# Attention scores on the whole TensorE array from hi/lo parts, and one run of value matmuls per head pair

## The chip, the cores and the metric

The kernel runs on one core of a Trainium2 chip. The metric is the device time of one execution in microseconds (us). A core has TensorE (PE in the profile; PEld is its weight load), VectorE (DVE), ScalarE (ACT), GpSimd (POOL) and SyncE (SP), which here issues nearly all DMAs; sixteen DMA engines carry them. SBUF is the working memory with 128 partitions, PSUM takes the results of TensorE, and HBM is the main memory.

## The reference, cut to what matters

Two layers over 256 context and 2048 latent tokens of width 1024. In each layer one projection feeds four head groups; two of them are attention, each with 4 query heads of width 64:

```
c: banded attention, 2 K/V heads (each serves 2 query heads)
   block of 128 queries x (up to 384 neighbours + 256 context keys), plus one sink logit per head
d: 2-D neighbourhood attention, 4 K/V heads
   128 queries (8 rows x 16 columns) x (12 or 16 rows of 32 columns = 384 or 512 keys + 256 context keys)
p = softmax(q.k * scale + bias);  o = p.v
```

Q and K are RMS-normalised per head (c also rotated by position). All of it is float32.

## The kernel before

Tokens go through in nine sub-blocks of 256 (s = 0 is the context). `project` multiplies a sub-block with a 256-column chunk of the weights as three float32r matmuls per 128 rows (hi*hi, hi*lo, lo*hi: lines 220 to 222, 48 matmuls of 256 columns per projection). The chunk names are `ckv` (K and V of group c), `dk`, `dv`, `cq`, `dq`; the results are stored to scratch in HBM and read back by the attention. Per layer the sub-blocks come in three groups of three (T1, T2, T3); in each the order is `bv`, `ckv`, `dk`, `dv`, every chunk for all three sub-blocks. For Q and K, `normrope` (line 367) normalises into the tile `e`, and `store_t` (line 331) transposes it on TensorE into PSUM (`pst`), copies it on ACT into `th`, and stores it: `ckv` one DMA of 128 KB, `dk` one of 256 KB with 128 partitions as its outermost dimension, `dq` four of 64 KB. `dv` is stored by two DMAs per sub-block (line 320), whose destination is a pattern of 2 x 64 x 256 elements. The tiles `e` and `ev` share the tag "e" of the pool `ev`, `nsq`, `th` and `xo` the tag "sq"; each tag has two buffers, taken in turn, and a tile may be written once the reader of the buffer's last tile, here its DMA, is done. PSUM for the projections (`pp`) has two buffers.

Attention (line 1180) is a list of items, one per head and block of 128 queries: 144 in layer 0, 128 in layer 1. Their order is given in `trunk`: neighbourhood (`na`) row groups 3 and 2, the banded (`swa`) blocks 10 to 15, then na 0, swa 0 to 3, na 1, swa 4 to 9; projections and the output projection stand between them and fill TensorE. A software pipeline (`pipeline`) issues for item i its scores, for i-1 the exponential, for i-2 the transposes of the probabilities, for i-3 the values. `attend` (line 822) computes the scores with float32 operands on half arrays: local keys in rows 0 to 63, context keys in rows 64 to 127 (`tile_position`). The tile scheduler that builds the program sorts the instructions of each engine by its own estimate of times. `head_out` (line 904) multiplies probabilities and values for two heads at once, head 0 in columns 0 to 63 of the array, head 1 in columns 64 to 127 (line 921). The scheduler is free to put other matmuls between these. One float32 matmul leaves two records in the trace, a float32r matmul or a transpose one. K is loaded by POOL's queue, Q by `load_q` with two DMAs into the two halves of the partitions, the same values twice.

Of the kernel before, what the change touches and what calls it, by code (L numbers as in the profile page):

```python
# [37 lines left out]
class Kern:  # L38
# [238 lines left out]
    def project(self, L, name, s, h, w):  # L277
# [32 lines left out]
        if name in ("av", "bv"):  # L310
            nc.scalar.copy(e, ps)
            nc.sync.dma_start((self.sav if name == "av" else self.sbv)[s], e)
        elif name == "dv":
            nc.scalar.copy(e, ps)
            dst = self.svd[s * SUB:s * SUB + SUB]
            if s == 0:
                nc.sync.dma_start(dst.rearrange("(t p) d -> p t d", p=128), e)
            else:
                for t in range(2):
                    nc.sync.dma_start(dst.rearrange("(c r) d -> r c d", r=4)[2 * t:2 * t + 2], e[:, t])  # L320
        elif name == "ckv":
# [3 lines left out]
            self.store_t(e, "ckv", s)  # L325
        else:
            w = {"cq": self.wcq, "dq": self.wdq, "dk": self.wdk}[name]
            self.normrope(ps, e, 4, w, s if name == "cq" else None)
            self.store_t(e, name, s)

    def store_t(self, e, name, s):
# [12 lines left out]
        if s > 0 and name == "dq":  # L344
            for i in range(n):
                nc.scalar.copy(x[:, i].rearrange("p (g r c) -> p r g c", g=4, r=4), p[:, i].rearrange("p (r g c) -> p r g c", g=4, r=4))
        elif s > 0 and name == "dk":
            nc.scalar.copy(x.rearrange("p i (c r) -> p i r c", r=4), p.rearrange("p i (r c) -> p i r c", r=4))
        else:
            nc.scalar.copy(x[:, 0:n], p[:, 0:n])  # L350
        if name == "cq":
            nc.sync.dma_start(self.sqc.rearrange("(i p) t -> p i t", p=128)[:, :, tok], x)
        elif name == "ckv":
            nc.sync.dma_start(self.skc.rearrange("g d t -> (g d) t")[:, tok], x[:, 0])
        elif name == "dk":
            nc.sync.dma_start(self.skd.rearrange("(i h) d t -> (h d) i t", i=2)[:, :, tok], x)
        else:
            for h in range(2):
                v = x[64 * h:64 * h + 64]
                for i in range(2):  # L360
                    if s == 0:
                        nc.sync.dma_start(self.sqx[:, i, :, h].rearrange("t d c -> d t c"), v[:, i].rearrange("d (t c) -> d t c", t=2))
                    else:
                        half = ((s - 1) % 2) * 64
                        nc.sync.dma_start(self.sqd[(s - 1) // 2, i, :, :, h, half:half + 64].rearrange("g d c -> d g c"), v[:, i].rearrange("d (g c) -> d g c", g=4))
# [449 lines left out]
    def load_q(self, pool, src, n):  # L815
# [4 lines left out]
        return q  # L820

    def attend(self, pool, rc, q, parts, a0, n, bias, nsink=None, split=False):

        nc = self.nc
        p = self.pS.tile([128, 1024], F32, tag="s", name="pse")
# [5 lines left out]
        so, pi = S[:, 0:n], p[:, a0:a0 + n]  # L833
# [16 lines left out]
    def transpose_p(self, pool, S, n, rc=None):  # L850
# [6 lines left out]
        for c0 in range(0, n, 3):  # L857
# [39 lines left out]

    def load_v(self, pool, tag, src, n):
# [28 lines left out]
    def swa(self, L, pool, jobs):  # L927
# [3 lines left out]
        sqc, svc = self.sqc, self.svc  # L931
        skc = self.skc.rearrange("g d t -> d g t")
# [3 lines left out]
        def prep():  # L936
            n = 128 * (top - base + 1)
            k = st["k"] = pool.tile([128, 2, 1024], F32, tag="k", name="kst", bufs=2)
            nc.gpsimd.dma_start(k[64:128, :, 0:256], skc[:, :, 0:256])
            nc.gpsimd.dma_start(k[0:64, :, 0:n], skc[:, :, 256 + 128 * base:256 + 128 * base + n])  # L940
            st["vc"] = self.load_v(pool, "vc", svc[0:256].rearrange("(n p) d -> p n d", p=128), 2)
            st["v"] = {}

        def front(j, h):
            g = h // 2
            k, vc = st["k"], st["vc"]
            if h == 0:
                st[j] = self.load_q(pool, sqc.rearrange("(h d) t -> d h t", d=64)[:, :, (j + 2) * 128:(j + 3) * 128], 4)
# [6 lines left out]
            q = st[j][:, h]  # L955
# [5 lines left out]
            ctx = (1, 512, 768, k[64:128, g, 0:256])  # L961
            if j < 0:
                S, *f = self.attend(pool, rc[:, h % 2:h % 2 + 1], q, [ctx], 512, 256, self.cmask[:, 384:640], ns)
# [3 lines left out]
            a0 = 512 - (k1 - k0)  # L967
# [3 lines left out]
            S, *f = self.attend(pool, rc[:, h % 2:h % 2 + 1], q, [(0, a0, 512, k[0:64, g, k0:k1]), ctx], a0, 768 - a0, bias, ns, j == 15)  # L971
# [13 lines left out]
    def na(self, L, pool, rg):  # L985
# [3 lines left out]
        svd, sqd = self.svd, self.sqd  # L989
# [4 lines left out]
        def prep(hp):  # L994
            st[hp] = self.na_keys(pool, hp, 256 + 64 * r0, ng)

        def front(hp, cg, i):
            c0 = CG_COL[cg]
            k, vc = st[hp]
            if i == 0:  # L1000
                st["q"] = self.load_q(pool, sqd[rg, hp, cg], 2)
# [4 lines left out]
            vs, q, rc = st["v"], st["q"][:, i], st["rc"]  # L1006
# [5 lines left out]
            kl = k[0:64, i].rearrange("p (n q) -> p n q", q=256)[:, 0:3, 4 * c0:4 * c0 + 128]  # L1012
            parts = [(0, 128, 512, kl)]
            if ng == 4:
                parts.append((1, 512, 640, k[64:128, i, 256 + 4 * c0:256 + 4 * c0 + 128]))
            parts.append((1, 128 + nloc, 384 + nloc, k[64:128, i, 0:256]))
            S, *f = self.attend(pool, rc[:, i:i + 1], q, parts, 128, nloc + 256, pool_st["b", i][:, a0:768])
# [13 lines left out]
    def na_keys(self, pool, hp, t0, ng):  # L1031

        nc = self.nc
        kt = self.skd[2 * hp:2 * hp + 2].rearrange("h d t -> d h t")
        k = pool.tile([128, 2, 768], F32, tag="k", name="kst", bufs=2, padded_shape=[128, 2, 1024])
        nc.gpsimd.dma_start(k[64:128, :, 0:256], kt[:, :, 0:256])
        if ng:
            nc.gpsimd.dma_start(k[0:64], kt[:, :, t0:t0 + 768])
        if ng == 4:
            nc.gpsimd.dma_start(k[64:128, :, 256:512], kt[:, :, t0 + 768:t0 + 1024])  # L1040
        vc = self.load_v(pool, "vc", self.svd[0:256, hp * 128:hp * 128 + 128].rearrange("(n p) d -> p n d", p=128), 2)
        return k, vc

    def na_ctx_rows(self, L, pool):

        nc = self.nc
        st = {}

        def prep(hp):
            st[hp] = self.na_keys(pool, hp, 0, 0)  # L1050

        def front(hp, t, i):
            k, vc = st[hp]
            if i == 0:
                st["q"] = self.load_q(pool, self.sqx[t, hp], 2)
                st["rc"] = self.sm.tile([128, 2], F32, tag="rc", name="rc", bufs=4)
            rc = st["rc"]
            S, *f = self.attend(pool, rc[:, i:i + 1], st["q"][:, i], [(1, 512, 768, k[64:128, i, 0:256])], 512, 256, self.cmask[:, 384:640])
# [51 lines left out]
    def scratch(self, L):  # L1110
# [11 lines left out]
        self.sqc = self.scr(f"qc{L}", [256, NT * 128])  # L1122
        self.skc, self.skd = self.scr(f"kc{L}", [2, 64, NT * 128]), self.scr(f"kd{L}", [4, 64, NT * 128])
        self.sqx, self.sqd = self.scr(f"qx{L}", [2, 2, 64, 2, 128]), self.scr(f"qd{L}", [4, 2, 4, 64, 2, 128])
# [257 lines left out]
```

## Time and profile before

| | |
|---|---|
| time, median of 3 runs | 3062.85 us (3062.26 to 3063.51) |
| the profiled execution | 3059.56 us, of which the span of its instructions is 3057.7 us |
| mean granted TensorE clock | 0.959 |
| busy: PE, PEld, DVE, ACT, POOL | 93%, 80%, 53%, 35%, 27% of the span |
| DMA | 458 MB, mean 150 GB/s, queues busy 49% of sixteen engines' span |

Shares are averages over stages. The attention takes about 770 to 1470 us (layer 0) and 2312 to 2930 us (layer 1); the projections with the gated linear attention of group a lie before them. A PE row gives start, length and what it computed; rows of TensorE overlap, so the cost of a matmul is the distance from its start to the next start, not its length.

### The profile page before, as it was taken

The page shows a single profiled execution, that of the slowest core. Times are in us where ns is not written, and L with a number is a line of the kernel's source. Part 1 is how long each engine was busy: PE and PEld are TensorE (multiplying, and loading weights), DVE is VectorE, ACT ScalarE, POOL GpSimd, SP SyncE. Part 2 cuts the span into 40 slices and gives each one's busy share as a digit, 9 for nine tenths or more (in the row PEclk, how much of TensorE's full clock was granted, in tenths as well). Part 3 has the DMA queues.
Part 4 walks back from the last instruction along what each step waited for, and adds up shares of the span by engine and source line. Part 5 has one row for each costly group of instructions (what it writes and reads, how often), then busy time and mean ns, then how long its engine had stood idle before and what let it go on. Part 6 is the DMA issues. An engine that isn't in the chain of part 4 may idle for free. (4 is left out here: it accounts for less than half of the span.)

```text
span 3057.7 us, 56121 instructions
## 1 busy us (share of the span) xinstructions
PE 2854.0 (93%) x21206; PEld 2447.1 (80%) x21206; DVE 1618.5 (53%) x3741; ACT 1073.4 (35%) x2344; POOL 836.8 (27%) x922
## 2 busy tenths in 40 slices
PE   5989979978999999999979989999889999999998
PEld 5879879967777777777879889899778777777788
DVE  7554864475455444545654553465564546455453
ACT  3333323322343332434224323343223444343332
POOL 3242322343222111311132432333342213111132
PEclk9989979989999999999989899899999999999999
DMA  8634634254654263542554664242546643446365
GB/s 265 196 110 149 190 110 128 91 175 145 179 155 136 83 189 109 166 133 92 191 159 148 195 183 142 87 132 89 165 148 188 175 130 110 148 127 187 110 189 188
DMA packets 476684, 458.05 MB, mean 150 GB/s; under 512 B 54763, under 2 KB 355565, under 8 KB 476013
## 3 DMA queue, kind: packets, MB, share of 16 engines
q1 hardware_dynamic: 472782, 440.66, 47.2%
q0 software_dynamic: 3616, 13.64, 1.9%
q8 instruction: 173, 2.83, 0.4%
q14 instruction: 113, 0.93, 0.1%
HBM read 339.56 MB, written 114.60 MB: 149 GB/s over the span
## 5 line engine op out<-in xcount | busy, mean ns | idle before, releaser
L220 PE MATMUL ps<-whi,hh 128*128 128x256 f32 x1968 | 587.3, 298 | 33.6 <-ACT hh L258 18.2
L222 PE MATMUL ps<-whi,hl 128*128 128x256 f32 x1968 | 584.2, 297 | 9.1 <-DVE hl L259 9.1
L221 PE MATMUL ps<-wlo,hh 128*128 128x256 f32 x1968 | 583.1, 296 | 6.8 <-PEq L639 6.8
L213 POOL TENSOR_TENSOR wlo<-wraw,whi 128x512 fp32r<-128x512 f32 x208 | 284.7, 1369 | 831.3 <-ACT whi L212 801.9
L220 PEld LDWEIGHTS ps<-whi,hh 128*128 128x128 f32 x1968 | 393.0, 200 | 46.9 <-ACT hh L258 20.1
L220 PE MATMUL ps<-hh,whi 128*128 128x256 f32 x1376 | 405.6, 295 | 5.9 <-DVE nsq L376 2.6
L222 PEld LDWEIGHTS ps<-whi,hl 128*128 128x128 f32 x1968 | 391.9, 199 | 21.8 <-DVE hl L259 12.9
L221 PE MATMUL ps<-hl,whi 128*128 128x256 f32 x1376 | 405.9, 295 | 0.0
L221 PEld LDWEIGHTS ps<-wlo,hh 128*128 128x128 f32 x1968 | 393.0, 200 | 15.1 <-issue 12.8
L222 PE MATMUL ps<-hh,wlo 128*128 128x256 f32 x1376 | 404.5, 294 | 0.0
L844 ACT ACTIVATE S<-S,am 128x641 f32<-128x641 f32 (+5 forms) x272 | 226.0, 831 | 502.7 <-DVE am L836 490.3
L212 ACT CAST whi<-wraw 128x512 fp32r<-128x512 f32 x416 | 242.9, 620 | 428.1 <-DMA wraw<-w_in 193.4
L220 PE MATMUL pso<-mh,whi 128*128 128x256 f32 x1088 | 320.4, 295 | 7.3 <-DVE xo L1106 5.0
L222 PE MATMUL pso<-mh,wlo 128*128 128x256 f32 x1088 | 319.0, 294 | 3.0 <-POOL wlo L213 1.9
L221 PE MATMUL pso<-ml,whi 128*128 128x256 f32 x1088 | 318.4, 293 | 0.0
L221 PEld LDWEIGHTS ps<-hl,whi 128*128 128x128 f32 x1376 | 264.8, 192 | 35.8 <-issue 35.5
L220 PEld LDWEIGHTS ps<-hh,whi 128*128 128x128 f32 x1376 | 264.7, 192 | 32.2 <-issue 24.3
L222 PEld LDWEIGHTS ps<-hh,wlo 128*128 128x128 f32 x1376 | 264.4, 192 | 26.9 <-issue 26.5
L213 DVE TENSOR_TENSOR wlo<-wraw,whi 128x512 fp32r<-128x512 f32 x208 | 192.9, 931 | 170.4 <-ACT whi L212 162.2
L191 POOL TENSOR_TENSOR rs<-ms,mhalf 128x8 f32<-128x8 f32 (+2 forms) x140 | 172.1, 1231 | 314.6 <-DVE ms L189 305.6
L830 PE MATMUL pse<-kst,q 64*128 64x256 f32 (+2 forms) x1184 | 243.8, 457 | 3.2 <-DVE am L836 2.3
L220 PEld LDWEIGHTS pso<-mh,whi 128*128 128x128 f32 x1088 | 213.0, 196 | 25.4 <-issue 19.5
(203 smaller groups left out, 5052.8 us busy)
## 6 DMA issues: line engine op xcount, KB each, us to landing
wraw<-w_in SPq DMA_DIRECT2D x288, 256.0 KB
wraw<-w_out SPq DMA_DIRECT2D x128, 256.0 KB
adaw<-ada_w SPq DMA_DIRECT2D x82, 256.0 KB
scr_g<-ev SPq DMA_DIRECT2D x68, 256.0 KB
g<-scr_g SPq DMA_DIRECT2D x34, 512.0 KB
y<-scr_y SPq DMA_DIRECT2D x34, 512.0 KB
bias<-nbias SPq DMA_DIRECT2D x48, 256.0 KB
scr_h<-x SPq DMA_DIRECT2D x22, 512.0 KB
```

What stands on the lines that cost most here:

```text
L191: nc.gpsimd.tensor_tensor(out=rs, in0=ms, in1=self.mhalf.to_broadcast([128, n]), op=ALU.pow)
L212: nc.scalar.copy(hi[:, k], raw)
L213: (nc.gpsimd if i % 4 else nc.vector).tensor_tensor(out=lo[:, k], in0=raw, in1=hi[:, k], op=ALU.subtract)
L220: nc.tensor.matmul(out, ah(k), bh(k), start=(k == 0), stop=False)
L221: nc.tensor.matmul(out, ah(k), bl(k), start=False, stop=False)
L222: nc.tensor.matmul(out, al(k), bh(k), start=False, stop=(k == KB - 1))
L830: nc.tensor.matmul(p[:, lo:hi], q[r], k, start=True, stop=True, tile_position=(64 * o, 0))
L844: nc.scalar.activation(out=S[:, 0:w], in_=S[:, 0:w], func=AF.Exp, scale=-1.0, bias=m[:, 0:1], accum_out=m[:, 1:2])
```

## The change

Scores: `store_t` becomes `split_t`. ACT writes hi = float32r(x), VectorE writes lo = x - hi (tile `tl`, tag "e"), and both are stored, so the scratch arrays of Q and K double. In attention, K is loaded with its hi part in partitions 0 to 63 and its lo part in 64 to 127; Q's hi part stands twice in one tile (`qa`), its lo part twice in another (`qb`). Per head and key range there are two whole-array float32r matmuls, qa and qb, instead of one float32 matmul on half an array. Q is loaded into a staging tile (`qs`, 2 buffers) and copied by ACT into a float32r tile (3 buffers; 4 before).

Values: the chunks are taken in the opposite order with head 1 first, under high priority. The copies of the transposed probabilities go to DVE for head 0 and to ACT for head 1; before, the first three chunks went to DVE and the rest to ACT.

```
-        x = self.ev.tile([128, 2, 256], F32, tag="sq", name="th")
+        hi = self.ev.tile([128, 2, 256], F32R, tag="sq", name="th")
+        lo = self.ev.tile([128, 2, 256], F32R, tag="e", name="tl")
...
+                nc.scalar.copy(hv[:, i], pv[:, i])
+                nc.vector.tensor_tensor(out=lv[:, i], in0=pv[:, i], in1=hv[:, i], op=ALU.subtract)
...
-            nc.sync.dma_start(self.skc.rearrange("g d t -> (g d) t")[:, tok], x[:, 0])
-            nc.sync.dma_start(self.skd.rearrange("(i h) d t -> (h d) i t", i=2)[:, :, tok], x)
+        for l, x in zip(range(2), (hi, lo)):
+            elif name == "ckv":
+                nc.sync.dma_start(self.skc[:, l, :, tok], x[:, 0])
+            elif name == "dk":
                 for i in range(2):
+                    nc.sync.dma_start(self.skd[2 * i:2 * i + 2, l, :, tok], x[:, i])
...
-        q = pool.tile([128, n, 128], F32, tag="q", name="q", bufs=4, padded_shape=[128, 4, 128])
-        for o in range(2):
-            self.nc.sync.dma_start(q[64 * o:64 * o + 64], src)
+        q = pool.tile([128, 2, 2, 128], F32R, tag="q", name="q", bufs=3)
+        st = pool.tile([128, 2, 2, 128], F32, tag="ks", name="qs", bufs=2)
+        self.nc.sync.dma_start(st, src.rearrange("d h l t -> d (h l t)").rearrange("(o d) x -> o d x", o=1).to_broadcast([2, 64, 512]))
+        self.nc.scalar.copy(q, st)
...
+            q = pool.tile([128, 4, 128], F32R, tag="q", name="q", bufs=3)
+            st = pool.tile([128, 4, 128], F32, tag="ks", name="qs", bufs=2)
+            for o in range(2):
+                self.nc.sync.dma_start(st[64 * o:64 * o + 64], src(d))
+            self.nc.scalar.copy(q, st)
...
-        for o, lo, hi, k in parts:
-            r = slice(64 * o, 64 * o + 64)
-            nc.tensor.matmul(p[:, lo:hi], q[r], k, start=True, stop=True, tile_position=(64 * o, 0))
+        for lo, hi, k in ((a0, 512, kloc), (512, 768, kc)):
+            if hi > lo:
+                nc.tensor.matmul(p[:, lo:hi], qa[:, h], k, start=True, stop=False)
+                nc.tensor.matmul(p[:, lo:hi], qb[:, h], k, start=False, stop=True)
...
-            if c0:
+            if rc is not None:
                 nc.scalar.copy(pt[:, 0:w], p[:, 0:w])
...
-            for c in range(n):
-                for x, h in enumerate((r[6], r)):
-                    nc.tensor.matmul(py[64 * x:64 * x + 64, 0:128], h[2][c], h[5][0][c], start=(c == 0), stop=(c == n - 1), tile_position=(0, 64 * x))
+            with self.tc.high_priority():
+                for c in range(n - 1, -1, -1):
+                    for x, h in ((1, r), (0, r[6])):
+                        nc.tensor.matmul(py[64 * x:64 * x + 64, 0:128], h[2][c], h[5][0][c], start=(c == n - 1), stop=(c == 0), tile_position=(0, 64 * x))
...
-        self.skc, self.skd = self.scr(f"kc{L}", [2, 64, NT * 128]), self.scr(f"kd{L}", [4, 64, NT * 128])
+        self.skc, self.skd = self.scr(f"kc{L}", [2, 2, 64, NT * 128]), self.scr(f"kd{L}", [4, 2, 64, NT * 128])
```

On TensorE, in banded attention of layer 1 (`pse` scores, `ppt` transposes, `py` values, `ps` filling projections), the order before for one head pair's end:

```order
L830 MATMUL pse<-kst,q 128x384
L830 MATMUL pse<-kst,q 128x256
L220 MATMUL ps<-hh_31404,whi 128x256
L921 MATMUL py<-pt,vd 64x128 x5
L921 MATMUL py<-pt,vc 64x128
L221 MATMUL ps<-hl_31405,whi 128x256
L222 MATMUL ps<-hh_31404,wlo 128x256
L220 MATMUL ps<-hh_31404,whi 128x256
L221 MATMUL ps<-hl_31405,whi 128x256
L222 MATMUL ps<-hh_31404,wlo 128x256
L862 MATMUL ppt<-idn,S 128x128 x5
L921 MATMUL py<-pt,vc 64x128 x3
```

and now:

```order
L960 MATMUL py<-pt,vc 64x128 x4
L960 MATMUL py<-pt,vd 64x128 x8
L890 MATMUL ppt<-idn,S 128x128 x2
L857 MATMUL pse<-kst,q 128x384
L858 MATMUL pse<-kst,q 128x384
L857 MATMUL pse<-kc,q 128x256
L858 MATMUL pse<-kc,q 128x256
L890 MATMUL ppt<-idn,S 128x128 x3
```

The value matmuls of a pair, before in several runs with other matmuls between them, stand together; in the whole list there were 456 such runs, and there are 136, one for each pair. Both lists hold 1360 value matmuls.

On SP's queue, in group T2 of layer 1 (stores of K and V), before:

```order
L354 DMA scr_kc<-th 128x256
L356 DMA scr_kd<-th 128x2x256
L211 DMA wraw<-w_in 128x512 x4
L356 DMA scr_kd<-th 128x2x256
L469 DMA scr_so_6<-rec 128x512
L320 DMA scr_vd<-ev 2x64x256 x2
L356 DMA scr_kd<-th 128x2x256
L320 DMA scr_vd<-ev 2x64x256 x4
```

and now, from the stores of the last `ckv` sub-block to half of those of the second `dk` sub-block:

```order
L363 DMA scr_kc<-th 2x64x256
L363 DMA scr_kc<-tl 2x64x256
L366 DMA scr_kd<-th 2x64x256
L366 DMA scr_kd<-tl 2x64x256
L366 DMA scr_kd<-th 2x64x256
L366 DMA scr_kd<-tl 2x64x256
L211 DMA wraw<-w_in 128x512
L479 DMA scr_so_6<-rec 128x512
L211 DMA wraw<-w_in 128x512 x3
L366 DMA scr_kd<-th 2x64x256
L366 DMA scr_kd<-tl 2x64x256
```

Each `dk` sub-block now has four stores and each `ckv` sub-block two, all with the pattern 2 x 64 x 256 that only `dv` had.

On ACT, at the end of the same kind of group (T1 of layer 1), with the semaphores that an instruction waits for, now:

```order
L314 COPY ev<-ps 128x512 [waits DVE_49]
L353 CAST th<-pst 128x4x64 [waits DVE_49]
L471 COPY rec<-po 128x256 [waits PE_49]
L442 COPY ktt<-pk 128x256 [waits PE_49]
L314 COPY ev<-ps 128x512 [waits DMAHW4_49,DMAHW7_49,DMAHW1_49,DVE_49]
L314 COPY ev<-ps 128x512 [waits DMAHW2_49,DMAHW3_49,PE_49,Activation_49]
L212 CAST whi<-wraw 128x512
```

The second `dv` copy (the first line 314 with DMA waits) takes the buffer of the last `tl` and so waits for its stores; the weight casts of the next chunk stand behind it on ACT.

## Rows read from the trace of the kernel before

**Rows 1.** The page: engine busy us (share of the span) and instructions.
```profile
PE 2854.0 (93%) x21206; PEld 2447.1 (80%) x21206; DVE 1618.5 (53%) x3741; ACT 1073.4 (35%) x2344; POOL 836.8 (27%) x922
```

**Rows 2.** Stretches: length, then busy us (instructions) of each engine, clock, DMA share, GB/s.
```profile
766.00:932.00 166.00, 163.25 (x1259) 127.46 (x1258) 80.87 (x192) 67.49 (x150) 42.78 (x51) 0.98 0.60 169
...
2312.00:2470.00 158.00, 157.19 (x1228) 122.85 (x1228) 81.26 (x186) 69.14 (x151) 43.47 (x48) 1.00 0.66 187
2470.00:2584.00 114.00, 114.00 (x873) 86.11 (x872) 59.10 (x143) 46.62 (x110) 28.61 (x50) 1.00 0.37 106
```

**Rows 3.** Timeline of PE around one item's scores: start us, length us, instruction, count.
```profile
2493.33 0.28 PE L222 MATMUL ps<-hh,wlo 128*128 128x256 f32 x1
2493.54 0.91 PE L830 MATMUL pse<-kst,q 64*128 64x384 f32 x4
2494.38 0.39 PE L220 MATMUL ps<-hh,whi 128*128 128x256 f32 x1
2494.61 0.28 PE L221 MATMUL ps<-hl,whi 128*128 128x256 f32 x1
2494.72 0.29 PE L222 MATMUL ps<-hh,wlo 128*128 128x256 f32 x1
```

**Rows 4.** Timeline of PE around a run of one value matmul.
```profile
2496.22 0.27 PE L866 MATMUL ppt<-idn,rd 128*128 128x128 f32 x1
2496.43 0.43 PE L921 MATMUL py<-pt,vd 128*64 128x128 f32 x2
2496.79 0.39 PE L221 MATMUL ps<-hl,whi 128*128 128x256 f32 x1
2497.01 0.28 PE L222 MATMUL ps<-hh,wlo 128*128 128x256 f32 x1
```

**Rows 5.** Timeline of PE around a run of nine value matmuls.
```profile
2499.96 0.71 PE L862 MATMUL ppt<-idn,S 128*128 128x128 f32 x5
2500.59 0.76 PE L921 MATMUL py<-pt,vd 128*64 128x128 f32 x9
...
2501.20 0.70 PE L921 MATMUL py<-pt,vc 128*64 128x128 f32 x7
2501.83 0.39 PE L220 MATMUL ps<-hh,whi 128*128 128x256 f32 x1
2502.05 0.28 PE L221 MATMUL ps<-hl,whi 128*128 128x256 f32 x1
```

**Rows 6.** PE by line and shape: count, busy us, mean ns, idle before.
```profile
L830 PE MATMUL pse<-kst,q 64*128 64x384 f32 x480 | 219.6, 538 | 3.2 <-DVE am L836 2.3 <-DMA kst<-scr_kd 0.8
...
L830 PE MATMUL pse<-kst,q 64*128 64x256 f32 x576 | 184.0, 419 | 0.0
...
L830 PE MATMUL pse<-kst,q 64*128 64x128 f32 x128 | 31.1, 322 | 0.0
```

**Rows 7.** Stretches in the stores of K and V, columns as in rows 2.
```profile
604.00:605.00 1.00, 1.00 (x10) 1.00 (x10) 0.00 (x0) 0.00 (x0) 0.00 (x0) 1.00 0.91 198
606.50:611.50 5.00, 5.00 (x45) 4.97 (x44) 0.28 (x1) 0.36 (x1) 0.00 (x0) 1.00 0.14 48
...
1918.00:1947.00 29.00, 28.90 (x235) 27.73 (x234) 9.92 (x18) 10.46 (x20) 8.82 (x6) 1.00 0.29 94
```

**Rows 8.** What line 320 (the stores of `dv`) kept waiting: us, times.
```profile
  ACT ev L314: 5.5, 2
```

**Rows 9.** SP's queue in group T2 of layer 1: start us, length us, DMAs.
```profile
1918.70 0.37 SPq L356 DMA_DIRECT2D scr_kd<-th  x1
...
1935.62 0.38 SPq L356 DMA_DIRECT2D scr_kd<-th  x1
1938.69 5.18 SPq L320 DMA_DIRECT2D scr_vd<-ev  x4
```

**Rows 10.** Nearest operations to the added ones: ns min/median/max, first and last start.
```profile
L293 DVE SCALAR_TENSOR_TENSOR ev<-ev,ps x68: 660/686/690, 720.8 to 2752.8; 128x512 f32<-128x512 f32 x68
...
L212 ACT CAST whi<-wraw x416: 598/619/696, 8.4 to 3047.5; 128x512 fp32r<-128x512 f32 x139
```

More of the change, by code (lines that the diff above doesn't have):

```diff
@@ L324, in project @@
             self.normrope(ps[:, :, 0:128], e[:, :, 0:128], 2, self.wck, s)
-            self.store_t(e, "ckv", s)
+            self.split_t(e, "ckv", s)
         else:
@@ L328, in project, with split_t @@
             self.normrope(ps, e, 4, w, s if name == "cq" else None)
-            self.store_t(e, name, s)
-    def store_t(self, e, name, s):
+            self.split_t(e, name, s)
+    def split_t(self, e, name, s):
         nc = self.nc
@@ L341, in store_t @@
                 nc.tensor.transpose(p[:, i, t * 128:t * 128 + 128], e[:, t, i * 128:i * 128 + 128], self.idn)
-        x = self.ev.tile([128, 2, 256], F32, tag="sq", name="th")
+        hi = self.ev.tile([128, 2, 256], F32R, tag="sq", name="th")
+        lo = self.ev.tile([128, 2, 256], F32R, tag="e", name="tl")
         tok = slice(s * SUB, s * SUB + SUB)
-        if s > 0 and name == "dq":
+        if s > 0 and name in ("dq", "dk"):
+            if name == "dq":
+                hv, lv = (x.rearrange("p i (g r c) -> p i r g c", g=4, r=4) for x in (hi, lo))
+                pv = p.rearrange("p i (r g c) -> p i r g c", g=4, r=4)
+            else:
+                hv, lv = (x.rearrange("p i (c r) -> p i r c", r=4) for x in (hi, lo))
+                pv = p.rearrange("p i (r c) -> p i r c", r=4)
@@ L345, in store_t @@
             for i in range(n):
-                nc.scalar.copy(x[:, i].rearrange("p (g r c) -> p r g c", g=4, r=4), p[:, i].rearrange("p (r g c) -> p r g c", g=4, r=4))
-        elif s > 0 and name == "dk":
-            nc.scalar.copy(x.rearrange("p i (c r) -> p i r c", r=4), p.rearrange("p i (r c) -> p i r c", r=4))
-        else:
[L350 to L353, printed above, removed]
-            nc.sync.dma_start(self.skc.rearrange("g d t -> (g d) t")[:, tok], x[:, 0])
-        elif name == "dk":
-            nc.sync.dma_start(self.skd.rearrange("(i h) d t -> (h d) i t", i=2)[:, :, tok], x)
-        else:
-            for h in range(2):
-                v = x[64 * h:64 * h + 64]
-                for i in range(2):
[L361 to L365, printed above, removed]
@@ new lines, in split_t @@
+                nc.scalar.copy(hv[:, i], pv[:, i])
+                nc.vector.tensor_tensor(out=lv[:, i], in0=pv[:, i], in1=hv[:, i], op=ALU.subtract)
+        else:
+            nc.scalar.copy(hi[:, 0:n], p[:, 0:n])
+            nc.vector.tensor_tensor(out=lo[:, 0:n], in0=p[:, 0:n], in1=hi[:, 0:n], op=ALU.subtract)
+        for l, x in zip(range(2), (hi, lo)):
+            x = x.bitcast(F32)
+            if name == "cq":
+                nc.sync.dma_start(self.sqc[l].rearrange("(i p) t -> p i t", p=128)[:, :, tok], x)
+            elif name == "ckv":
+                nc.sync.dma_start(self.skc[:, l, :, tok], x[:, 0])
+            elif name == "dk":
+                for i in range(2):
+                    nc.sync.dma_start(self.skd[2 * i:2 * i + 2, l, :, tok], x[:, i])
+            else:
+                for i in range(2):
+                    for h in range(2):
+                        v = x[64 * h:64 * h + 64, i]
+                        if s == 0:
+                            nc.sync.dma_start(self.sqx[:, i, :, h, l].rearrange("t d c -> d t c"), v.rearrange("d (t c) -> d t c", t=2))
+                        else:
+                            half = ((s - 1) % 2) * 64
+                            nc.sync.dma_start(self.sqd[(s - 1) // 2, i, :, :, h, l, half:half + 64].rearrange("g d c -> d g c"), v.rearrange("d (g c) -> d g c", g=4))
@@ L896, in pipeline, with kv_tiles @@
                 res[i][3]()
+    def kv_tiles(self, pool, kt, vt, h0, t0, n):
+        kc = pool.tile([128, 2, 256], F32R, tag="kc", name="kc", bufs=2)
+        self.load_k(pool, kc, kt, h0, 0, 256)
+        kst = None
+        if n:
+            kst = pool.tile([128, 2, 1024], F32R, tag="kst", name="kst", bufs=2)
+            self.load_k(pool, kst, kt, h0, t0, n)
+        return kc, self.load_v(pool, "vc", vt[0:256, h0 * 64:h0 * 64 + 128].rearrange("(n p) d -> p n d", p=128), 2), kst
     def load_v(self, pool, tag, src, n):
@@ L930, in swa @@
         st = {}
-        sqc, svc = self.sqc, self.svc
-        skc = self.skc.rearrange("g d t -> d g t")
+        sqc, skc, svc = self.sqc, self.skc, self.svc
         lat = [j for j in jobs if j >= 0]
@@ L936, in prep @@
         def prep():
[L937 to L941, printed above, removed]
+            n = top - base + 1
+            st["k"] = self.kv_tiles(pool, skc, svc, 0, 256 + 128 * base, 128 * n)
             st["v"] = {}
@@ L954, in front @@
                             st["v"][b + x] = v[:, x]
-            q = st[j][:, h]
+            qa, qb = st[j]
             if h % 2 == 0:
@@ L988, in na @@
         st, pool_st = {}, self.bias
-        svd, sqd = self.svd, self.sqd
+        skd, svd, sqd = self.skd, self.svd, self.sqd
         r0, r1 = RG_ROWS[rg]
@@ L1029, in na @@
                 for a in ((hp, cg, i) for hp in range(2) for cg in range(4) for i in range(2))]
[L1031 to L1042, printed above, removed]
     def na_ctx_rows(self, L, pool):
```

56 lines of the change are left out of this document (30 added, 26 removed).

## The prediction

> **What bounds the kernel now.** I read four views in this order: the page, the stretches, the timeline of TensorE, the timeline of the stores. The page [rows 1] shows PE busy for 93% of the span, which alone says little. The stretches say more: in attention PE is busy 163.25 of 166, 157.19 of 158 and 114.00 of 114 us at a granted clock of 0.98 to 1.00 (the 2.4 GHz level), DVE and ACT about half of that [rows 2]. So there the sum of what stands in PE's list is the time, and work taken off that list comes straight off the end, as long as nothing else becomes late. The candidates for that are the DMA engines, at 0.60 and 0.66 in the neighbourhood stretches and 0.37 in a banded one.
>
> The timeline then gives the price of the two things that change. Filling matmuls start 0.11 to 0.12 us apart. From the last one before the scores (2493.33) to the second one after them (2494.61) are 1.28 us; less two ordinary distances the scores cost 1.04 us, although the array only streams 384 columns [rows 3]. A run of one value matmul costs 2497.01 - 2496.22 - 0.11 (transpose) - 0.12 = 0.56 us [rows 4]. A run of nine (eighteen records, two of the four rows of it are left out) costs 2502.05 - 2499.96 - 5 x 0.11 - 0.12 = 1.42 us [rows 5]; five transposes start 0.11 apart, (0.71 - 0.27)/4. Nine matmuls are five steps, as two heads' matmuls go side by side. So a run costs 0.345 us for entering and leaving the divided array, and 0.215 us a step.
>
> **The change part by part.** The trace's own execution is 3059.6 us; it is 3.3 us under the median of 3062.85, which I add at the end.
>
> *Scores.* 272 items, about 1.0 us each (items with context keys alone have less; their share is small [rows 6]): 272 us go. Added are whole-array float32r matmuls over 2 x (local + 256) columns: 176 items with 384 local keys, 64 with 512, 16 with 256, 16 with none, 348,160 columns in all. The nearest row is the filling float32r matmul of 256 columns at 0.12 us [rows 3], so 1360 x 0.12 = 163 us. Gain 109 us. 384 and 512 columns are not in the trace: at 0.11 per 256 the gain is 122, and if a wider float32r matmul fell back to what the old scores cost it is 0.
>
> *Values.* The PE lists have 456 runs with 827 steps before and 136 runs with 680 steps now. Before: 456 x 0.345 + 827 x 0.215 = 335 us; now 47 + 146 = 193 us. Gain 142 us. The reversed order of chunks means that a run waits once, for the last copy of head 1's probabilities, with the rest of PE's list queued behind it. PE's list has some ten or more fillers and the next scores between the last transpose and the run, over 2 us, against a copy of fewer columns than the 512 that take ACT 0.62 us [rows 10], so I cost that at nothing beyond the waits below.
>
> Together 251 us, 1.85 us for each of 136 head pairs.
>
> *Stores of K.* Here the change pays. The stores of `dv`, with a pattern of 2 x 64 x 256, run alone at a DMA share of 0.14, two of sixteen engines, and at 48 GB/s, though several are queued; one microsecond in which a `dk` store (128 partitions outermost) is in flight shows 0.91 and 198 GB/s [rows 7]. So patterns that begin with 2 all share the same two engines. `ckv` now makes two such stores (256 KB, 5.5 us at 48 GB/s) and `dk` four (512 KB, 10.9 us), `dv` two as before (5.5 us). In group T2 of layer 1 three `dk` start at 1918.70, and the second `dv` store follows at 1938.69 [rows 9], 20 us later. `tl` shares two buffers with `ev`, and the second `dv` copy takes the buffer of the last `tl`, so it now waits for three `dk` and one `dv` on those two engines: 3 x 10.9 + 5.5 = 38.2 us, about 5 us of other DMAs on them (0.29 of 20 us [rows 7], less their own part), and about 2 us to land (an estimate): 45 us, 25 late. Behind it on ACT stand the weight casts of the next chunk, and PE runs dry when its second PSUM buffer is full, one projection of 48 x 0.12 = 5.8 us later: 20 us. Before, such stores held ACT up for 5.5 us in all [rows 8]. The other five groups have the sub-blocks further apart or, in T1, a context sub-block without this pattern; I take 15 us each on average, 90 us, between 30 (only the backlog of the last stores counts) and 150 (25 each).
>
> *Loads of Q.* A neighbourhood pair's Q now comes in one DMA of 256 KB whose source begins with a repeat of 2. No row shows such a load. If it spreads like the others it costs nothing; if it goes like the stores with 2 in front it takes 5.5 us of two engines. I take the second, the row with the same leading 2. Row groups 3 and 2 stand together, 16 pairs: 88 us. The two engines also carry their sixteenth of all else: 0.60 x 166 = 100 and 0.66 x 158 = 104 us by busy share, or, at the 24 GB/s that one engine of the two moves, 169 x 166/384 = 73 and 187 x 158/384 = 77 us; I take 86 and 90. K, doubled, and the old Q loads, gone, cancel. Two loads land before the start (-11). That is 163 and 167 us, where PE would need 163 - 30 = 133 and 157 - 30 = 127: 30 and 40 us lost. In row groups 0 and 1 half of eight loads are issued in the banded stretch ahead, with its share of 0.37 [rows 2]: 5 us each for four. Sum 90 us; between 0 and 235 (no load early, shares as in rows 2: some 70 in each double stretch, 25 in each single one).
>
> The Trainium skill, "DMA: Bandwidth & Descriptors", section "Why a DMA increments its semaphore by 16 and not by 1", says that a DMA uses the largest number of engines, up to 16, that divides the outermost size (not 1) of both patterns, and its "Rules for kernel authors" name a leading repeat of c copies as confined to at most c engines. By this rule the two Q terms above hold; without it they are zero and the sum is 90 us lower. The trace agrees for the stores of `dv`: 48 GB/s at a share of 0.14.
>
> *Small things.* 70 subtractions on DVE at 0.69 us (48 us) and 136 Q copies on ACT at 0.62 us (84 us) [rows 10] lie beside PE, DVE being at 53% and ACT at 35% [rows 1]; where DVE leads, ahead of attention, some of the 48 shows: 10 us, between 0 and 48. The first scores of a Q tile now wait for DMA, then ACT, then PE, and the score bank still has one buffer: 15 us of new waits, between 0 and 40.
>
> Sum: 3059.6 - 109 - 142 + 90 + 90 + 15 + 10 = 3014; with 3.3 for the median **3017 us**, 1.5% faster: a gain of 251 of which 205 is given back to two DMA engines and small waits.
>
> **The rivals.** *A: the two-engine transfers hide.* For it: `dv` stores of this kind held up only 5.5 us in all [rows 8], Q has five buffers on its way, and the wait for a store costs only if PE has nothing else. Against it: before, one chunk in four did it, now three. With the Q loads hidden 3017 - 90 = 2927, with the stores hidden too 2837; I take 2910 as its middle.
>
> *B: slower, the two engines lead.* Place: the groups T1 to T3 and the double neighbourhood stretch. Price: 150 for the stores, some 160 for Q (half the early loads do not come early, and every other DMA of SP's queue passes the same two engines and arrives late), 25 for small things: 335 - 251 = 84 slower, 3147; it decides from a loss of 251 on. For it: SP and ACT take their work in order, so one late store stops weights and Q as well. Against it: late transfers also thin out what the two engines have to carry.
>
> *C: the scores do not get cheaper*, because wide float32r matmuls cost as much as the old ones: 3017 + 109 = 3126. *D: gain and loss cancel* within 0.2%, 6 us, about what a measurement of this kernel can tell from no change.
>
> **How the numbers follow.** Forecast 0.45, its own range 2960 to 3056 (the terms for stores and Q some 40 us either way). A 0.20, B 0.25, C 0.03, D 0.07. Faster: forecast and A, 0.65. Same: most of D, 0.06. Slower: B, C and the rest, 0.29. For 8 in 10 the range leaves out half of A below and a third of the slower cases above: 2895 to 3125.
>
> **What would show it.** In the new profile the scores should stand in four records per item at 0.15 to 0.18 us apart for 384 columns, with no gap to the fillers, and values in one run of 1.4 to 1.7 us. Stretches with only `dk` stores should show a share near 0.14 and 48 GB/s for 10 us and more; ACT's `ev` copy and DVE's `tl` should wait for stores; PE's idle time should grow between 150 and 620 and in the same part of layer 1. If a neighbourhood stretch of 16 pairs takes about 135 us instead of 165, Q's loads are spread or hidden, and A is right; if it takes over 190, B. The prediction is wrong at its root if PE is still near 100% busy in attention and the total is not shorter there.

## The result and the profile after

The changed kernel takes 3179.57 us (median of 4 runs, 3175.36 to 3186.22) against 3063.18 for the kernel before: the ratio is 1.0381, 95% interval 1.0362 to 1.0400. It is 3.8% slower. I had forecast 3017, 1.5% faster, with a range to 3125; rival B (slower, two engines lead) stood at 3147 with a chance of 0.25.

The page of the changed kernel, first line, as in [rows 1]:

```profile
PE 2695.1 (85%) x21078; PEld 2530.5 (80%) x21078; DVE 1619.3 (51%) x3835; ACT 1146.6 (36%) x2504; POOL 837.2 (26%) x914
```

PE has 159 us less to do (2854.0 before), in a span that is 115.5 us longer: it is not the work that grew but the gaps. Gaps between the starts of PE's matmuls that are longer than 0.7 us, less an ordinary 0.12 us each, sum to 204 us before and 491 now. PE's list itself became as short as forecast. Its timeline around one item's scores (start, length, instruction, count):

```profile
1063.30 0.36 PE L222 MATMUL ps<-hh,wlo 128*128 128x256 f32 x1
1063.50 0.34 PE L857 MATMUL pse<-kst,q 128*128 128x384 f32 x1
1063.67 0.34 PE L858 MATMUL pse<-kst,q 128*128 128x384 f32 x1
1063.85 0.28 PE L857 MATMUL pse<-kc,q 128*128 128x256 f32 x1
1063.97 0.28 PE L858 MATMUL pse<-kc,q 128*128 128x256 f32 x1
1064.09 0.28 PE L220 MATMUL ps<-hh,whi 128*128 128x256 f32 x1
1064.20 0.28 PE L221 MATMUL ps<-hl,whi 128*128 128x256 f32 x1
```

Matmuls of 384 columns start 0.17 to 0.18 us apart, those of 256 columns 0.12. From the last filler to the second one after are 0.90 us; less two ordinary distances 0.66, where [rows 3] had 1.04. And a pair's values, one run:

```profile
1061.66 0.28 PE L221 MATMUL ps<-hl,whi 128*128 128x256 f32 x1
1061.87 0.66 PE L960 MATMUL py<-pt,vc 128*64 128x128 f32 x8
1062.35 0.82 PE L960 MATMUL py<-pt,vd 128*64 128x128 f32 x12
1063.11 0.44 PE L890 MATMUL ppt<-idn,S 128*128 128x128 f32 x2
```

Twenty records (ten matmuls, five steps) take 1063.11 - 1061.66 - 0.11 = 1.34 us, where the forecast had 1.42.

The time went into gaps at the two places that rival B names, and at a third, the single row groups. First the stores of K. Stretches of the changed kernel in group T3 of layer 0, where the stores of `dk` run and those of `dv` queue behind them, columns as in [rows 2]:

```profile
655.00:660.00 5.00, 3.06 (x26) 2.77 (x24) 0.56 (x3) 0.00 (x0) 0.00 (x0) 1.00 0.14 50
660.00:665.00 5.00, 0.00 (x0) 0.00 (x0) 0.00 (x0) 0.00 (x0) 0.00 (x0) 0.67 0.14 48
665.00:670.00 5.00, 2.86 (x13) 2.86 (x14) 0.00 (x0) 0.58 (x1) 0.00 (x0) 0.50 0.14 48
```

Ten microseconds and more at a share of 0.14 and 48 GB/s, as with `dv` alone in [rows 7], and in the middle of it the busy time of every engine in the row is 0.00. Behind the gap PE's granted clock is 0.50, the 1.2 GHz level, so a gap costs more than its length.

Second, attention. I count from the start of an item's exponential to that of a later item's, so the items between are the same in every kernel. The filling matmuls among them are not: the three stretches hold 526, 550 and 505 before, 567, 594 and 580 in the change, so 5 to 9 us of the change's stretches, at 0.11 to 0.12 us a matmul, are more filling work. The stretches are items 0 to 31 and 40 to 71 of layer 0 (the double neighbourhood stretch; row group 0 with the banded items that lead to it) and the first 32 items of layer 1. Before:

```profile
775.00:936.00 161.00, 158.25 (x1221) 122.21 (x1221) 81.84 (x192) 67.39 (x150) 41.47 (x47) 0.98 0.59 169
974.00:1136.00 162.00, 157.39 (x1153) 117.43 (x1152) 75.80 (x173) 61.66 (x144) 27.39 (x49) 0.97 0.45 133
2323.00:2476.00 153.00, 153.00 (x1197) 117.48 (x1196) 82.55 (x191) 69.93 (x153) 42.39 (x48) 1.00 0.64 182
```

The same items in the changed kernel:

```profile
861.00:1028.00 167.00, 144.03 (x1199) 135.47 (x1200) 81.17 (x201) 77.94 (x169) 42.26 (x46) 0.92 0.64 187
1062.00:1229.00 167.00, 138.27 (x1204) 131.27 (x1204) 76.56 (x179) 68.61 (x158) 31.99 (x49) 0.90 0.55 158
2445.00:2617.00 172.00, 144.96 (x1203) 136.33 (x1204) 79.99 (x196) 79.95 (x174) 42.97 (x47) 0.92 0.64 189
```

PE was nearly full there; now it is idle for 23, 29 and 27 us, and its clock lower, so each stretch is longer although its scores and values take less. The mean DMA share, 0.55 to 0.64, shows no full engine: it is a mean over sixteen. Who waits for whom, from the waits of the changed kernel (us, times, longest):

```profile
DVE S L864 <- DMA bias<-nbias: 107.9, 29, 10.7
ACT q L835 <- DMA qs<-scr_qd: 64.9, 11, 11.2
ACT ev L314 <- DMA scr_kd<-tl: 57.4, 5, 13.7
DVE tl L354 <- DMA scr_kd<-tl: 30.8, 5, 8.2
```

The third and fourth line are the waits that the prediction named for the stores. The first is the telling one: the largest wait is not for Q but for the bias, a load that the change did not touch. Before:

```profile
DVE S L836 <- DMA bias<-nbias: 7.5, 3, 5.0
```

### The profile page after: what moved, and what is told of

It reads as the page before. It is cut to its first block, busy times and chain, and to the rows that moved or that the text cites. A ratio compares the mean times of both kernels' runs of the same rounds, so it can differ in the third digit from the quotient of the medians.

```text
span 3173.2 us, 56054 instructions
## 1 busy us (share of the span) xinstructions
PE 2695.1 (85%) x21078; PEld 2530.5 (80%) x21078; DVE 1619.3 (51%) x3835; ACT 1146.6 (36%) x2504; POOL 837.2 (26%) x914
## 5 line engine op out<-in xcount | busy, mean ns | idle before, releaser
L220 PE MATMUL ps<-whi,hh 128*128 128x256 f32 x1968 | 601.5, 306 | 100.1 <-ACT ev L314 44.2
L222 PE MATMUL ps<-whi,hl 128*128 128x256 f32 x1968 | 594.9, 302 | 12.4 <-DVE hl L259 12.4
L221 PE MATMUL ps<-wlo,hh 128*128 128x256 f32 x1968 | 592.8, 301 | 4.6 <-PEq L649 3.8
L220 PEld LDWEIGHTS ps<-whi,hh 128*128 128x128 f32 x1968 | 407.5, 207 | 112.0 <-ACT ev L314 46.0
L222 PEld LDWEIGHTS ps<-whi,hl 128*128 128x128 f32 x1968 | 405.5, 206 | 18.1 <-DVE hl L259 15.5
L221 PEld LDWEIGHTS ps<-wlo,hh 128*128 128x128 f32 x1968 | 407.6, 207 | 7.4 <-issue 4.2
L890 PE MATMUL ppt<-idn,S 128*128 128x128 f32 x1360 | 250.7, 287 | 103.0 <-DVE pt L900 45.6
L220 PEld LDWEIGHTS ps<-hh,whi 128*128 128x128 f32 x1376 | 272.3, 198 | 4.7 <-DVE nsq L386 3.3
L221 PEld LDWEIGHTS ps<-hl,whi 128*128 128x128 f32 x1376 | 272.0, 198 | 1.3 <-issue 1.1
L890 PEld LDWEIGHTS ppt<-idn,S 128*128 128x128 f32 x1360 | 161.7, 145 | 128.9 <-DVE pt L900 48.6
```

The source lines that it names most:

```text
L220: nc.tensor.matmul(out, ah(k), bh(k), start=(k == 0), stop=False)
L221: nc.tensor.matmul(out, ah(k), bl(k), start=False, stop=False)
L222: nc.tensor.matmul(out, al(k), bh(k), start=False, stop=(k == KB - 1))
L890: nc.tensor.transpose(p[:, i], S[:, (c0 + i) * 128:(c0 + i + 1) * 128], self.idn)
```

## The experiments

The theory: DMAs whose pattern begins with 2 all run on the same two engines, and what is late is everything that passes them. The main rival: the new chains (DMA, ACT, PE ahead of the scores; ACT's last copy ahead of the values) make PE wait, whatever engines carry the data.

**a1_q64.** Q's loads as two DMAs of 64 partitions:

```
-        self.nc.sync.dma_start(st, src....to_broadcast([2, 64, 512]))
+        for o in range(2):
+            self.nc.sync.dma_start(st[64 * o:64 * o + 64], src)
```

> The changed kernel with each neighbourhood load of Q made as two DMAs of 64 partitions in place of one whose source begins with a repeat of 2; nothing else differs. Theory (the DMAs that begin with 2 crowd two engines): attention, which did not get shorter, loses most of its idle time, some 150 to 200 us: 2980 to 3030. Rival 1 (only the stores of K count): within 15 us of 3180. Rival 2 (the added chain DMA, ACT, PE ahead of the scores and the single run of values make PE wait, whatever engines carry the load): within 30 us of 3180, with the same idle time in attention.

Measured 2981.57 us (2975.69 to 2985.05), 198 less than the change. The stretches of the same items:

```profile
845.00:986.00 141.00, 135.35 (x1224) 128.08 (x1224) 83.15 (x204) 79.49 (x172) 43.37 (x46) 1.00 0.86 236
1019.00:1151.00 132.00, 128.04 (x1185) 122.21 (x1185) 74.02 (x180) 68.48 (x157) 31.49 (x49) 1.00 0.70 198
2333.00:2471.00 138.00, 134.19 (x1216) 127.16 (x1217) 82.72 (x196) 80.59 (x175) 43.45 (x47) 1.00 0.88 247
```

The three are 26, 35 and 34 us shorter (their filling matmuls differ by 2 us of work at most), PE is idle for only 4 to 6 us of each at a clock of 1.00, and the DMA share has gone *up*, to 0.70 to 0.88, with the same bytes in less time. The wait for the bias, untouched here too, falls from 107.9 to 32.8 us:

```profile
DVE S L865 <- DMA bias<-nbias: 32.8, 13, 4.3
ACT q L836 <- DMA qs<-scr_qd: 31.0, 10, 6.4
```

Rivals 1 and 2 of this run fall.

**a2_k64.** K's stores of 64 partitions:

```
-                nc.sync.dma_start(self.skc[:, l, :, tok], x[:, 0])
+                for h in range(2):
+                    nc.sync.dma_start(self.skc[h, l, :, tok], x[64 * h:64 * h + 64, 0])
...
-                for i in range(2):
-                    nc.sync.dma_start(self.skd[2 * i:2 * i + 2, l, :, tok], x[:, i])
+                for h in range(2):
+                    nc.sync.dma_start(self.skd[h::2, l, :, tok].rearrange("i d t -> d i t"), x[64 * h:64 * h + 64])
```

> The changed kernel with the stores of the parts of K made per head of 64 partitions (four DMAs per dk step as before the edit, four for ckv where it has two) in place of patterns that begin with 2. Theory: the groups T1 to T3 of both layers lose the lag that they gained, 70 us in each layer: about 3040; attention stays as it is. Rival 1 (the stores hide, Q counts): within 15 us of 3180. Rival 2 (the lag in these groups comes from 70 added subtractions and copies on DVE and ACT): within 30 us of 3180.

Measured 3057.04 us (3048.28 to 3068.88), 122.5 less. The first exponential of layer 0 starts at 797 us, against 861 in the change (775 before); from the last one of layer 0 to the first of layer 1 it is 838 us, against 891 (851 before). Attention keeps its losses, 166, 167 and 175 us for the three stretches. Both rivals of this run fall; the theory's 3040 was 17 us low. The wait behind the third line above falls to 15.9 us:

```profile
ACT ev L314 <- DMA scr_kd<-tl: 15.9, 4, 5.5
```

**a3_q64_k64.** Both edits.

> Both of these edits. Theory: the sum of the two gains, about 2850 (the list of PE is 250 us shorter, minus some 25 us of new waits and 15 for DVE and ACT), idle time of PE back near the 204 us that the kernel before has in gaps. Rivals that leave the cost to the new chains: above 3100.

Measured 2884.37 us (2881.39 to 2888.20), ratio to before 0.9426 (0.9411 to 0.9442). The rivals fall; the time is 34 us above the theory's number. PE's gaps sum to 257 us, still above the 204 of before. Behind Q's fix, K's is worth 97 us; behind K's, Q's is worth 173.

**a4_values** and **b1_scores64**, the two halves of the change apart. The first is the kernel before with the edit of the values:

```
-            for c in range(n):
-                for x, h in enumerate((r[6], r)):
+            with self.tc.high_priority():
+                for c in range(n - 1, -1, -1):
+                    for x, h in ((1, r), (0, r[6])):
...
-            if c0:
+            if rc is not None:
```

The second is a3 with exactly that edit undone.

> The kernel before with the edit of the values alone (one run per head pair, last chunk first, all copies of head 1's probabilities on ACT); its scores, Q and K are as before. Theory (a run costs 0.345 us to enter and leave plus 0.215 a step): 142 us less, about 2920. Rival (the run waits for its last copy and PE with it, so what is saved on entering is idle instead): 3040 to 3080.

> The scores alone with all transfers spread: the changed kernel with 64-partition Q loads and K stores, and with the values' runs and copies as they were before. Theory (the two parts add): the values alone took 85 us off the kernel before, all together 174, so the scores should be worth 89 here: about 2969. By the prediction's sum for the scores (109 less 25 of small waits) 2974. Rival (the two parts overlap, either one alone frees the same wait of DVE's reduction for the score bank): below 2940 here, since each alone would then be worth more than in the sum.

Values alone: 2973.02 us (2965.34 to 2978.72), 85 less than before, where theory had 142 and the rival none. Scores alone, with spread transfers: 2971.80 (2959.29 to 2975.59), 82.5 less. The two parts add: 167.5 us apart, 174 together; b1's rival (below 2940) falls. I summed PE's list in the attention stretches of the kernel before and of these two (each run from the end of the filler ahead to the filler behind, the median of each shape by its count): the values go from 323.5 to 176.9 us, the scores from 276.7 to 161.5. So the list shrinks by 147 and 115 us, as the sum had it (142 and 109); 62 and 32 us of it don't reach the end. For the values, the waits of PE itself (us, times, longest) in the run with the values alone show where most of it stands:

```profile
PE pse L830 <- DVE am L836: 21.3, 16, 4.1
PE py L922 <- ACT pt L870: 9.7, 6, 2.5
PE ppt L862 <- DVE pt L872: 9.5, 4, 5.7
PE ppt L862 <- DVE rc L847: 6.3, 3, 3.4
```

In the kernel before, the first of these reads

```profile
PE pse L830 <- DVE am L836: 2.3, 3, 1.0
```

and the other three come to 0.6 us. So 19 of the 62 us are waits of the scores for their bank, 15 waits of the transposes, and 10 the run of values waiting for ACT's last copy. PE, quicker by a run, seems to come back before DVE has read out the one score bank; that is a reading of these waits, not a test of it.

**b2_addq** and **b2_addq16.** The kernel before, with only the suspected cost added: 256 KB more per Q load, into a tile that nothing reads, once with a repeat of 2 in front, once in 64-partition DMAs:

```
+        if n == 2:
+            z = pool.tile([128, 512], F32, tag="qz", name="qz", bufs=2)
+            for o in range(2):
+                self.nc.sync.dma_start(z[:, 256 * o:256 * o + 256], src.rearrange("d h t -> d (h t)")....to_broadcast([2, 64, 256]))
```

> The kernel before with only the suspected cost added: beside each neighbourhood Q load two more DMAs of 128 KB whose source begins with a repeat of 2, into a tile that nothing reads. No engine waits for the data; only SP waits for the two buffers. Theory (two engines are filled and all else that passes them comes late): 80 to 160 us slower than before, 3140 to 3220, with idle time of PE in attention, where there was next to none. Rival 1 (what hurt was the wait for Q itself, on ACT, ahead of the scores): within 20 us of 3058. Rival 2 (any 256 KB more per pair would do it, bytes and not engines): as slow as the run with the same bytes in 64-partition DMAs.

> The control to that: the same 256 KB more per pair into the same unread tile, as four DMAs of 64 partitions. Theory: within 15 us of 3058. Rival 2 (bytes): as slow as its sister.

With two in front 3331.01 us (3329.25 to 3335.90), ratio 1.0909 (1.0880 to 1.0937): 277 slower, far more than expected. With the same bytes spread 3072.11 (3071.02 to 3079.20), 18 slower, a little over the 15 expected. Both rivals fall: nobody needs these data, and the bytes are the same. What waits, in the first:

```profile
DVE S L840 <- DMA bias<-nbias: 158.0, 18, 30.3
ACT ev L292 <- DMA scr_g<-ev: 115.6, 5, 51.2
```

and in the second:

```profile
DVE S L840 <- DMA bias<-nbias: 22.3, 12, 5.6
ACT ev L292 <- DMA scr_g<-ev: 4.1, 4, 2.7
```

Other transfers come late, one of them by 51 us. Why this costs more than the change's own Q loads isn't settled. The engines' work doesn't explain it: the added loads have 1 KB packets, twice as many as the change's, and all packets of that size together took 3109 us for 2292 before, which is 6.0 us of each of the two engines for one pair, against 5.8 in the change (b3 below). But this run adds a second cost, which its expectation mentions and does not price: SP itself stood for the two buffers of the added tile, and behind it every later load of its queue,

```profile
SPq L823 <- DMA qz<-scr_qd: 71.9, 33, 3.9
```

against 2.5 us in 4 times at the same line of the second. How much of the 277 us that is, no run separates.

**b3_q2act.** a2 with Q's loads in the change's form, from ACT's queue (`nc.scalar` for `nc.sync`).

> The changed kernel with spread K stores, and the Q loads with the repeat of 2 as in the change but issued from ACT's queue in place of SP's. Theory (the pattern picks the engines, the queue does not matter): within 30 us of the run with spread K stores alone, 3057. Rival (SP's queue, in which each such load holds up the next transfers in order): most of 170 us comes back, 2880 to 2930.

Measured 3055.22 us (3049.13 to 3069.47), a2's time. The order of SP's queue doesn't set the time; the rival falls. It does set who waits: the bias, 110.9 us in a2, waits less, and ACT's copy of Q, 77.4 us in a2, more:

```profile
ACT q L836 <- DMA qs<-scr_qd: 87.4, 18, 11.7
DVE S L865 <- DMA bias<-nbias: 45.7, 14, 7.3
```

So much of the bias's lateness seems to have come through SP's queue, behind Q's loads. And as these loads now have a queue of their own, the page prices them (packets, MB, share of 16 engines):

```profile
q10 hardware_dynamic: 8840, 17.83, 1.6%
```

1.6% of 16 x 3058 us is 783 us of engine, by two engines and 68 loads 5.8 us a load; the sum had 5.5.

**c1_qkv64, c2_copies, c3_allact, c4_bufs.** a3 with the stores of `dv` spread too; that with the copies of the probabilities as before the change; with all of them on ACT; and c1 with a buffer more for Q and for its loads:

```
                 for t in range(2):
-                    nc.sync.dma_start(dst.rearrange("(c r) d -> r c d", r=4)[2 * t:2 * t + 2], e[:, t])
+                    for r in range(2):
+                        nc.sync.dma_start(dst.rearrange("(c r) d -> r c d", r=4)[2 * t + r], e[64 * r:64 * r + 64, t])
```

> The changed kernel with Q loads and K stores spread, and now also the stores of dv (there in the kernel before too) made as DMAs of 64 partitions, four for two. Theory: these 64 stores fill the same two engines for 2.7 us each, but with the stores of K gone from there few waits are left: 0 to 20 us less than 2884. Rival (the two engines were full in these groups before the change too): 40 us less or more.

> As that, with the copies of the probabilities as before the change (the first three chunks of each head on DVE, the rest on ACT) and the values still one run per pair. With the values alone the list of PE got 147 us shorter, the time only 85, and the waits ahead of the scores for DVE's reduction rose from 5 to 47 us. Theory (head 0's five copies in a row on DVE delay the reduction that frees the one score bank): 20 to 40 us less than its sister. Rival (the bank is late because PE is faster, whoever copies): within 10 us. Rival 2 (the run now waits for DVE's copies of head 1 as well): 10 us slower or more.

> As that, with all copies of the probabilities on ACT, so that DVE has only the reductions, the reciprocals and the products here. Theory (DVE's copies delay the score bank): 20 us less than the first of these or more, unless ACT's exponentials, 40% busy as the mean, come late in turn. Rival (the bank is late because PE is faster): within 10 us, or slower by ACT.

> The first of these with one more buffer for Q's parts (4 in place of 3) and for what is loaded for them (3 in place of 2). In the spread kernel ACT's copy of Q waited 43 us, 28 times, until PE's scores gave a buffer back, with the exponentials queued behind it. Theory (that wait delays ACT, but PE has fillers): within 15 us of its sister. Rival (ACT's order sets the scores): 15 us less or more.

Measured 2855.23 us (2853.60 to 2860.23), 2865.12, 2861.27 and 2847.68 (2841.72 to 2853.55). Spreading `dv` is worth 29 us, between theory and rival. The theory on the copies falls: with them shared out as before it is 10 us slower, on the line between its two rivals, with all on ACT 6, within its rival's 10, and the scores wait longer for DVE's reduction, not shorter. PE's wait in c1 and in c2:

```profile
PE pse L860 <- DVE am L867: 18.3, 12, 4.5
```

```profile
PE pse L860 <- DVE am L867: 33.9, 16, 5.3
```

In c3 it is 32.4. (The 5 and 47 us in c2's expectation count each such wait twice, at the weight load and at its matmul; PE's own are 2.3 and 21.3.) With PE's waits for the copies of the transposed probabilities the three come to 49, 52 and 46 us: whoever copies, the wait changes its place and hardly its size. So the bank isn't late for the copies; that it is late because PE returns earlier remains, but was only argued. A second score buffer wasn't tried. With one more buffer it is 7.5 us less than c1, as the theory had it. The version with one more buffer beats both kernels: ratio 0.9318 (0.9295 to 0.9342), 6.8% faster than before.

**d1_bc_bufs, d2_bc_bufs5, d3_all_bufs5.** The change itself with 4 and 3, and with 5 and 3 buffers for Q's parts and its loads (3 and 2 in the change); and c1 with 5 and 3.

> The changed kernel, with its loads and stores as in the change, and one more buffer for Q's parts (4) and for what is loaded for them (3). Theory (the single row groups lose because their Q loads cannot be issued ahead): 20 to 50 us less than 3180, the gain in these groups. Rival (the two engines are full whenever the loads come): within 15 us of 3180.

> The same with 5 and 3 buffers. Theory: 40 to 75 us less than 3180, more of the loads being issued in the banded stretches. Rival: within 15 us of 3180.

> The kernel with Q, K and dv all spread, with 5 and 3 buffers. With 4 and 3 it took 2848, with 3 and 2 it took 2855. Theory (with spread loads the buffers hardly matter): 2835 to 2855. Rival (ACT's wait for a Q buffer still sets PE's scores): below 2835.

Measured 3180.69 us (3173.88 to 3182.94), 3205.26 (3199.15 to 3209.95) and 2863.19 (2857.41 to 2872.01). The theory of d1 and d2 falls: more buffers for Q gain nothing in all, and with five it is 26 us slower. Items 40 to 71 of layer 0 do get shorter, 167 us, 153, 151, but items 0 to 31 longer, 167, 179, 184. That two full engines make one stretch pay for what another is spared would fit this, but isn't shown. For d3 neither range held: it is slower than with four buffers, and why is open.

## Why the prediction was wrong, by its steps

*The bound and the gain on PE* were right: 147 and 115 us came off its list (142 and 109). *"Small things"* was mis-sized. The sum took 25 us; both parts together gave 174 us (3058.2 to 2884.4) where the sum, without the transfers, had 226. Of the 62 us that the values alone fell short, 44 stand in new waits of PE: 19 ahead of the scores, for the one bank that the 15 us of "new waits" named, 15 ahead of the transposes, which no term had, and 10 ahead of the values' run, where the prediction cost the wait for ACT's last copy at nothing.

*Stores of K* was right in place, mechanism and nearly in size: 90 forecast, 97 or 122 measured (behind Q's fix, or alone), through the very wait that was named. What each of the six groups lost, 20 or 15 us in the sum, was not measured by itself.

*Loads of Q* is the step that failed: 90 us forecast, 173 to 198 measured. Its price per load, 5.5 us of two engines, was right (5.8), and so was its sum for the double stretches: it gave 163 and 167 us, and they took 167 and 172; the loss is 27 us in layer 0 and 34 in layer 1 (change less a1), where 30 and 40 were forecast. Some of that closeness is luck: 12 loads were issued inside each stretch, not 14 (70 us of the two engines, not 77), and their sixteenth of all else was 98 and 101 us, not 86 and 90 (0.64 x 16 x 167 = 1710, less 12 x 2 x 5.8 = 139, over 16). It failed in the sentence on row groups 0 and 1, "half of eight loads are issued in the banded stretch ahead, with its share of 0.37": 5 us each for four. The loads do come early: in each of the four, five of the eight are issued before the row group's first exponential. But early loads were not cheap. By the items during which they are issued (40 to 71 and 88 to 111; in layer 1 192 to 215 and 216 to 239) the four lost 35, 22, 14 and 26 us: some 96, not 20, and near the 25 each that the prediction kept for loads that do not come early. From the first issue of such a group to 11 us after the last (the longest wait for such a load is 11.2 us) the rows of the changed kernel are

```profile
1090.00:1184.00 94.00, 70.84 (x596) 66.34 (x594) 38.82 (x84) 35.25 (x80) 17.72 (x25) 0.87 0.53 154
1319.00:1405.00 86.00, 69.73 (x579) 65.57 (x578) 34.32 (x97) 33.88 (x82) 15.67 (x20) 0.92 0.53 167
2681.00:2756.00 75.00, 69.08 (x629) 65.36 (x623) 37.75 (x99) 33.58 (x80) 16.79 (x26) 0.98 0.49 147
2833.00:2926.00 93.00, 70.68 (x615) 65.80 (x613) 36.41 (x89) 33.37 (x75) 15.19 (x25) 0.94 0.57 163
```

In the first, 0.53 x 16 x 94 = 797 us of engine; Q's eight loads are 8 x 2 x 5.8 = 93 of it, the rest is 704 / 16 = 44 for each engine. The two carry 44 + 46 = 90 us in 94. The other three come to 86 of 86, 77 of 75 and 94 of 93: full while the loads run, by the same kind of sum as in the double stretches. The share there is 0.49 to 0.57, not the 0.37 of the banded stretch before the change. Over the whole of items 40 to 71 it is (0.55 x 16 x 167 - 93) / 16 + 46 = 132 us of 167, so a sum over that stretch would not have shown it. The profiled executions of the change and a1 differ by 190 us; the 33 outside these stretches lie ahead of layer 0's attention (16), between the layers (15) and elsewhere (2).

The parts add up, from 3017: 52 (gain on PE, 226 to 174) + 108 (Q, 90 to 198) + 7 (K behind it, 90 to 97) - 5 (base: the kernel before took 3058.2 beside these runs, 3062.9 in the forecast) = 3179. They do so by construction, since K's and Q's parts are differences of the same runs.

*The rivals.* B had the mechanism, at 3147; its place lacked the single row groups. A fell, since neither the loads nor the stores hid: taking them off the two engines gave 173 to 198 and 97 to 122 us back. C fell: an item's scores cost 0.66 us in the rows above, and 384 columns 0.17 to 0.18. The rule of the Trainium skill ("DMA: Bandwidth & Descriptors", section "Why a DMA increments its semaphore by 16 and not by 1"), that a DMA uses the largest number of engines, up to 16, that divides the outermost size of both patterns, agrees with the packets of the change, a1, a2 and b3 (last section): two engines for a leading 2, sixteen for 64 partitions.

## What to carry to other kernels

Make the sum for the busiest two engines, not for the mean of sixteen: shares of 0.49 to 0.57 held two full ones, and in items 40 to 71 spreading the same bytes raised the mean from 0.55 to 0.70; the whole kernel got 198 us faster. The wait then also appears at a load that nobody changed (here the bias), and which load it hits depends on the queue: on a queue of their own the Q loads cost the same time, with less than half of the bias's wait. Make the sum for the time in which the loads run, not for a whole stage, and don't take early loads as cheap. Where a pattern would begin with a repeat of 2 or a 2, two DMAs of 64 partitions move the same bytes over all sixteen.

## What the runs showed of the hardware

How many engines a DMA uses can be counted on the page. The rows of the hardware queue in the change, a1 and a2 (packets, MB, share of 16 engines):

```profile
q1 hardware_dynamic: 518398, 474.47, 49.5%
```

```profile
q1 hardware_dynamic: 520438, 474.48, 53.4%
```

```profile
q1 hardware_dynamic: 520486, 474.48, 51.5%
```

The bytes agree, the packets don't: a1 has 2040 more, which is 68 x (2 x 16 - 2), and a2 2088, which is 36 x (2 x 16 - 2) for `ckv` and 72 x (16 - 2) for `dk`. So each DMA leaves one packet more per engine that it uses: two for the pattern that begins with 2, sixteen for 64 partitions. The queue row of b3 says the same: 8840 packets are 68 x 128 for the data and 68 x 2. And what such loads cost is not in proportion to the engines' work: 136 of them with 128 KB, added to the kernel before without a reader, cost 277 us, in a run in which SP also stood 72 us for their buffers; the same bytes spread cost 18.
